# First feed-forward block on TensorE: operand places in SBUF, the order of its opening, and eight modulation sums in another stage

## The chip, the cores and the metric

The kernel runs on one core of a Trainium2 chip as one program. Five engines work beside each other: TensorE (PE, matmuls), VectorE (DVE), ScalarE (ACT), GpSimd (POOL) and SyncE (SP), whose queue starts nearly all loads. Each engine runs its own instructions in order and waits on semaphores for the others. SBUF holds 128 partitions; PSUM takes the matmuls' sums in banks. The metric is the time of one execution on the device in microseconds (us).

## The reference

The model has two layers on 512 tokens and a context of 256, with 1024 features. Layer 0 mixes with a Fourier and Hyena mixer, layer 1 with attention. Each layer ends in a gated feed-forward block (FFN) with a convolution of three taps:

```python
def _adaln(cond, w_mod, b_mod):
    mod = jax.nn.silu(cond) @ w_mod + b_mod
    return jnp.split(mod[:, None, :], 6, axis=-1)

def _conv_ffn(h, w_up, conv_w, conv_b, w_down):
    gate, val = jnp.split(h @ w_up, 2, axis=-1)
    return (jax.nn.silu(_dwconv3(gate, conv_w, conv_b)) * val) @ w_down

for i in range(DEPTH):
    sh1, sc1, g1, sh2, sc2, g2 = _adaln(c, w_mod[i], b_mod[i])
    ...
    x = x + g1 * yx
    x = x + g2 * _conv_ffn(_modulate(_rms_norm(x, norm2[i]), sh2, sc2), *ffn)
    if not last:
        ctx = ctx + cg1 * yc
        ctx = ctx + cg2 * _conv_ffn(_modulate(_rms_norm(ctx, norm2[i]), csh2, csc2), *ffn)
```

The change lies in the FFN of layer 0, over tokens and context together (768 columns), and in the modulation sums (`_adaln`) of layer 1, which are computed while that FFN runs. What is computed stays the same.

## The kernel before

Features lie on the partitions and tokens along the free axis. Every float32 product is made of three matmuls (`mm3`, lines 335 to 337): each operand is split into a high part (ACT, line 309) and the rest (DVE, line 314), and high x high, low x high and high x low are summed in a bank. So a moving operand has tiles named with h and l, and a weight tile likewise: `wh`/`wl` (1024 columns wide), `bh`/`bl` (512 wide).

`up0` is the FFN of layer 0. Its input after the norm is `h0h`, `h0l`, `h1h`, `h1l`: four feature blocks of 128 in each, 768 columns. There are 22 blocks of 128 hidden features. The first five are computed plainly, the later 17 with seven products per block instead of eight, in the manner of Strassen: feature halves and column halves (384 each) form two-by-two blocks, P1 to P7 are the products, and T1, T2, T4 (and T3 in place of `h0`'s second half) are sums of input blocks, made once on DVE. A product is twelve matmuls of 384 columns.

Hidden blocks are gathered in six groups (`GROUPS0`). For the first five, the down product (`DN`, `DL`) reads the activations `act0` to `act5` and the weights `bh`/`bl`, in matmuls of 384 columns, and is added to the residual in DRAM (`XA`, `XD`). The sixth group has six blocks and is written out in Python behind the table: its matmuls have 256 columns, its weights are `wh`/`wl` and `k3h` to `k7l`, and its outputs go to the residual tiles `xr` (line 1833), whose squares (line 444) and sums (line 451) form the next norm: column sums on PE (line 457), reciprocal root on DVE (lines 462 to 353), spreading on PE (line 475).

All engines follow an order that is written out: `UP0_ORDER` is a table of tokens, each the name of a step and its block. `LG` and `LV` load a block's gate and value weights; `HG`, `DG`, `H1`, `D1` and the like split weights; `S1` to `S4` form sums of weights; `CV` to `MU` are the convolution and the gate; `AH`, `AL` split the activation; `LW`, `HW`, `DW` load and split down weights. `LM:i` loads one row block of the modulation matrix into a raw buffer, and `GV:i` forms its sum on DVE (line 420 for each condition, then line 421). Raw buffers (`wr`, three, and `wx`, two) are shared by `LG`, `LV`, `LW` and `LM`; a step takes the buffer that became free first, and SP waits until its last reader is done. There are 56 modulation sums left when `up0` begins; the last 40 need one condition alone. The table has numbers 0 to 47; `GEMV0 = 48` says that the last eight are formed in the sixth group, by `more` between the outputs.

The opening of `up0` stands ahead of the table: two outputs, (0, q = 0) and (0, q = 1), eight pieces each, beside which the context's norm ends (`take`, `f2`, `a2`).

Where tiles lie follows from the order of allocation and from small pad tiles (`hpad`, `tpad`, `bpad`, `apad`). Places modulo 512 bytes, per partition: `h0` 64, `h1` 128, T1 192, T2 256, T4 320, `act0` to `act5` 128, 192, 256, 320, 384, 448; weights `wh`/`wl` and `k3` to `k7` 256; `bh`/`bl` 384, 448 and 0. In the second FFN the moving operands lie at 448 and the weights at 256.

Of the kernel before, what the change touches and what calls it, by code (L numbers as in the profile page):

```python
# [30 lines left out]
GEMV0 = 48  # L31
# [119 lines left out]
LV:1 LG:2 LV:2 XS:0 LM:0 LG:3 EA:0 GB:0 GV:0 LM:1 VB:0 HV:1 EB:0 DV:1 CV:0 LV:3 CX:0 GB:1 HG:2 GV:1 CC:0 LM:2 VA:1 DG:2 HV:2 SI:0 DV:2 LG:4 EA:1 EB:1  # L151
MU:0 LM:3 GV:2 AH:0 VB:1 AL:0 LV:4 GV:3 CV:1 SG:2 HG:3 CX:1 LM:4 DG:3 CC:1 LW:0.0 SI:1 GV:4 SV:2 HV:3 EB:2 MU:1 EA:2 LW:0.1 HW:0.0 DV:3 AH:1 AL:1 LM:5
DW:0.0 CV:2 LW:0.2 HW:0.1 CX:2 DW:0.1 CC:2 LG:5 SG:3 HG:4 GV:5 SI:2 HW:0.2 MU:2 LM:6 DG:4 AH:2 AL:2 LV:5 DW:0.2 LW:0.3 GV:6 SV:3 HV:4 EA:3 EB:3 CV:3
DV:4 LM:7 CX:3 LW:0.4 CC:3 SI:3 GV:7 SG:4 HG:5 MU:3 LM:8 DG:5 AH:3 AL:3 T1:0 GV:8 TH1:0 SV:4 EA:4 EB:4 CV:4 CX:4 LG:6 T2:0 CC:4 TH2:0 TL1:0 SI:4 T1:1
DN:0.0 DL:0.0 MU:4 TH1:1 T2:1 DN:0.1 XA:0.0 HW:0.3 XD:0.0 TL1:1 TH2:1 DW:0.3 T4:0 LV:6 DN:0.2 XA:0.1 TL2:0 HA:5 XD:0.1 TH4:0 T4:1 TL4:0 TH4:1 P1:5
HW:0.4 DA:5 XA:0.2 TL4:1 P2:5 E1:5 S1:5 XD:0.2 TL2:1 S3:5 DN:0.3 T3:0 AH:4 H1:5 D1:5 HA:6 XA:0.3 S2:5 P5:5 DW:0.4 LM:9 XD:0.3 S4:5 LW:0.5 T3:1 H4:5
P4:5 E5:5 HG:6 D4:5 TH3:1 TH3:0 TL3:1 P6:5 LM:10 TL3:0 HW:0.5 DG:6 DN:0.4 E2:5 GV:9 P3:5 DA:6 XA:0.4 LW:0.6 C1:5 XD:0.4 S1:6 DW:0.5 P7:5 S3:6 LM:11
C2:5 H1:6 S2:6 P1:6 E3:5 V2:5 HW:0.6 D1:6 P2:6 V1:5 LW:0.7 AL:4 GV:10 CV:5 P5:6 P4:6 DW:0.6 LG:7 CX:5 LM:12 DN:0.5 HW:0.7 S4:6 CC:5 H4:6 GV:11 SI:5
E1:6 HG:7 DN:0.6 XA:0.5 D4:6 LV:7 XD:0.5 MU:5 LW:1.0 C1:6 E5:6 DW:0.7 AH:5 P6:6 DG:7 LM:13 XA:0.6 HA:7 AL:5 XD:0.6 P3:6 E2:6 GV:12 HW:1.0 DN:0.7 C2:6
LW:1.1 DA:7 CV:6 GV:13 P7:6 XA:0.7 XD:0.7 HW:1.1 P1:7 CX:6 E3:6 LM:14 V2:6 CC:6 P2:7 V1:6 SI:6 S1:7 E1:7 MU:6 S3:7 AH:6 DW:1.0 H1:7 AL:6 DN:1.0 LW:1.2  # L160
D1:7 DL:1.0 S2:7 DW:1.1 LG:8 P5:7 XA:1.0 S4:7 LM:15 GV:14 H4:7 XD:1.0 P4:7 E5:7 HW:1.2 HG:8 D4:7 DN:1.1 LV:8 DW:1.2 LW:1.3 DG:8 LM:16 C1:7 P6:7 XA:1.1
GV:15 XD:1.1 HA:8 P3:7 E2:7 HW:1.3 DW:1.3 LW:1.4 DA:8 DN:1.2 LM:17 C2:7 S1:8 CV:7 GV:16 P7:7 XA:1.2 HW:1.4 XD:1.2 S3:8 LG:9 P1:8 E3:7 V2:7 H1:8 S2:8
# [12 lines left out]
H4:13 MU:12 LV:14 P2:13 E1:13 D4:13 AH:12 DN:3.0 AL:12 HG:14 LW:3.3 GV:31 DL:3.0 C1:13 LM:32 P5:13 XA:3.0 HW:3.2 XD:3.0 DW:3.2 P4:13 E5:13 LM:33 GV:32
P6:13 HA:14 DA:14 LW:3.4 S1:14 DN:3.1 E2:13 S3:14 GV:33 P3:13 XA:3.1 LG:15 HW:3.3 XD:3.1 DW:3.3 DN:3.2 H1:14 C2:13 LM:34 CV:13 D1:14 DG:14 P7:13
XA:3.2 CX:13 HW:3.4 XD:3.2 P1:14 E3:13 V2:13 S2:14 V1:13 LV:15 S4:14 P2:14 CC:13 H4:14 DW:3.4 E1:14 D4:14 LW:3.5 DN:3.3 SI:13 HG:15 MU:13 LM:35 DG:15
AH:13 P5:14 HA:15 GV:34 XA:3.3 C1:14 XD:3.3 LW:3.6 P4:14 E5:14 DA:15 GV:35 P6:14 HW:3.5 S1:15 LM:36 DW:3.5 S3:15 LW:3.7 DN:3.4 E2:14 AL:13 S2:15 S4:15
GV:36 P3:14 XA:3.4 HW:3.6 XD:3.4 LG:16 DW:3.6 P7:14 H1:15 C2:14 LV:16 CV:14 D1:15 P1:15 E3:14 V2:14 H4:15 LM:37 CX:14 P2:15 V1:14 CC:14 D4:15 SI:14
DN:3.5 E1:15 MU:14 LW:4.0 HG:16 C1:15 AH:14 DG:16 P5:15 HA:16 XA:3.5 AL:14 GV:37 XD:3.5 P4:15 E5:15 LM:38 DN:3.6 HW:3.7 DW:3.7 DA:16 LW:4.1 S1:16  # L180
S3:16 P6:15 XA:3.6 S2:16 GV:38 HW:4.0 XD:3.6 P3:15 E2:15 DW:4.0 LM:39 S4:16 LW:4.2 P7:15 H1:16 C2:15 CV:15 D1:16 DN:3.7 E3:15 V2:15 H4:16 LG:17 CX:15
V1:15 CC:15 P1:16 XA:3.7 D4:16 SI:15 XD:3.7 HW:4.1 P2:16 MU:15 LM:40 E1:16 DW:4.1 AH:15 GV:39 LV:17 P5:16 HG:17 AL:15 LW:4.3 DG:17 DN:4.0 E5:16 DL:4.0
C1:16 GV:40 P4:16 XA:4.0 LM:41 HW:4.2 XD:4.0 DW:4.2 DN:4.1 HA:17 LW:4.4 DA:17 S1:17 GV:41 P6:16 XA:4.1 S3:17 LM:42 HW:4.3 XD:4.1 S2:17 P3:16 DW:4.3
E2:16 S4:17 LG:18 DN:4.2 H1:17 C2:16 GV:42 CV:16 D1:17 LV:18 P7:16 XA:4.2 CX:16 LW:4.5 HW:4.4 XD:4.2 DW:4.4 P1:17 E3:16 V2:16 LM:43 H4:17 V1:16 CC:16
P2:17 D4:17 E1:17 SI:16 LW:4.6 MU:16 DN:4.3 HG:18 C1:17 AH:16 DG:18 GV:43 P5:17 HA:18 XA:4.3 DA:18 LM:44 AL:16 XD:4.3 P4:17 E5:17 S1:18 S3:18 P6:17
S2:18 HW:4.5 DW:4.5 S4:18 LW:4.7 GV:44 DN:4.4 E2:17 LG:19 P3:17 XA:4.4 HW:4.6 XD:4.4 DW:4.6 P7:17 H1:18 C2:17 LM:45 CV:17 D1:18 P1:18 E3:17 V2:17
# [66 lines left out]
class Builder:  # L253
# [1097 lines left out]
    def layer0(self):  # L1351
# [40 lines left out]
    def up0(self, x, H, hh, hl, steps, first, gl):  # L1392
# [30 lines left out]
        with self.tc.manual_schedule(engines={ENG.PE, ENG.DVE, ENG.Activation, ENG.SP, ENG.Pool}):  # L1423
# [1585 lines left out]
```

## Time and profile before

| what | us |
|---|---|
| three runs | 1535.95, 1524.69, 1538.45 |
| median | 1535.95 |
| the profiled execution's own time | 1526.98 |
| its span, first to last instruction | 1525.2 |

The span is cut into stages by the line and tile names: mixer up to about 340 us, opening and up stage of the first FFN to 831.6, its sixth group to 894.8, then attention and the second FFN. Matmuls are pipelined, and the profile's end of a matmul is modelled, so the pace of a row of matmuls is read from the spacing of their starts. A line of the views gives busy time of an instruction group, the mean of one, and the idle time of its engine ahead of it with what ended it. A wait is named by the engine that came last.

### The profile page before, as it was taken

How to read it: one execution, taken by the hardware profiler on the slowest of the kernel's cores; microseconds unless marked ns; L12 is line 12 of the kernel's file. 1: busy time of each engine (PE TensorE's matmuls, PEld its weight loads, DVE VectorE, ACT ScalarE, POOL GpSimd, SP SyncE). 2: the span in 40 equal slices, each digit the busy share in tenths (PEclk: the TensorE clock that was granted, in tenths of full speed). 3: DMA queues.
4: the chain of work that ended last, by engine and by line, in shares of the span. 5: the costliest groups of instructions: out<-in, count | busy, mean ns of one | idle time of the engine just before them, and what ended most of it. 6: DMA issues, size and time to landing. Idle time of an engine off the chain costs nothing.

```text
span 1525.2 us, 24578 instructions
## 1 busy us (share of the span) xinstructions
PE 1483.3 (97%) x9668; PEld 1346.8 (88%) x9668; DVE 1269.3 (83%) x2150; ACT 773.4 (51%) x1236; POOL 129.5 (8%) x150
## 2 busy tenths in 40 slices
PE   7999999999999999999999888999999999999998
PEld 4778888889999999999999877766558999999998
DVE  5799978888989898878787667999987899898883
ACT  4362235424445555555555235988964556555551
POOL 0022126000000111010100000111120000000000
PEclk9999999999999999999999989999999999999999
DMA  9336512454535767776763720000015123332322
GB/s 342 137 109 215 184 61 70 145 186 180 162 86 136 188 173 181 190 178 169 185 161 104 240 73 32 10 15 6 10 43 179 63 77 127 110 115 94 119 91 98
DMA packets 66370, 192.30 MB, mean 126 GB/s; under 512 B 7499, under 2 KB 14989, under 8 KB 65229
## 3 DMA queue, kind: packets, MB, share of 16 engines
q1 hardware_dynamic: 60493, 174.99, 34.4%
q0 software_dynamic: 5760, 15.73, 6.9%
q8 instruction: 76, 1.25, 0.3%
q14 instruction: 41, 0.34, 0.1%
HBM read 166.05 MB, written 24.64 MB: 125 GB/s over the span
## 4 chain that ended last, share of the span: by engine, by line
PE 85%; DVE 8%; ACT 2%; issue 2%; DMA 2%; POOL 1%; SPq 0%; ACTq 0%; DVEq 0%; POOLq 0%
PE bank L337 16%; PE bank L335 16%; PE bank L336 16%; PE mm L335 5%; PE mm L336 4%; PE mm L337 4%; PE pv L2282 3%; PE ms L337 3%; PE ms L335 3%; PE ms L336 3%; DVE junk L420 2%; PE s L335 2%; PE pv L2293 1%; PE s L337 1%; PE s L336 1%
## 5 line engine op out<-in xcount | busy, mean ns | idle before, releaser
L309 ACT ACTIVATE wh<-wr 128x1024 fp32r<-128x1024 f32 (+2 forms) x150 | 148.1, 989 | 167.1 <-PE bank L336 53.3
L314 DVE TENSOR_TENSOR wl<-wr,wh 128x1024 fp32r<-128x1024 f32 (+2 forms) x150 | 171.3, 1145 | 19.5 <-ACT wh L309 18.8
L335 PE MATMUL bank<-act,wh 128*128 128x256 f32 x406 | 113.3, 279 | 0.0
L337 PE MATMUL bank<-act,wl 128*128 128x256 f32 x406 | 113.2, 279 | 0.0
L336 PE MATMUL bank<-act,wh 128*128 128x256 f32 x406 | 113.0, 278 | 0.0
L420 DVE SCALAR_TENSOR_TENSOR junk<-wr,sb 128x1024 bf16<-128x1024 f32 x83 | 101.7, 1225 | 8.3 <-DMA wr<-wmodT 8.3
L337 PE MATMUL bank<-act,bl 128*128 128x384 f32 x256 | 86.5, 338 | 0.5 <-DVE bl L314 0.5
L336 PE MATMUL bank<-act,bh 128*128 128x384 f32 x256 | 86.4, 337 | 0.0
L335 PE MATMUL bank<-act,bh 128*128 128x384 f32 x256 | 86.1, 336 | 0.0
L337 PEld LDWEIGHTS bank<-act,wl 128*128 128x128 f32 x406 | 77.1, 190 | 0.1
L336 PEld LDWEIGHTS bank<-act,wh 128*128 128x128 f32 x406 | 77.1, 190 | 0.0
L335 PEld LDWEIGHTS bank<-act,wh 128*128 128x128 f32 x406 | 77.1, 190 | 0.0
L1773 POOL DMA_DIRECT2D xq<-st x40 | 34.8, 870 | 485.3 <-ACT st L1768 485.3
L337 PE MATMUL bank<-h0h,wl 128*128 128x384 f32 x216 | 72.8, 337 | 1.4 <-DVE wl L314 1.4
L335 PE MATMUL bank<-h0h,wh 128*128 128x384 f32 x216 | 72.8, 337 | 0.0
L336 PE MATMUL bank<-h0l,wh 128*128 128x384 f32 x216 | 72.6, 336 | 0.0
L2234 ACT ACTIVATE S<-s,rks 128x512 f32<-128x512 f32 x96 | 63.1, 688 | 12.7 <-PE s L337 6.3
L335 PE MATMUL mm<-hh,wh 128*128 128x512 f32 x152 | 62.5, 411 | 5.5 <-ACT wh L309 3.0
L336 PE MATMUL mm<-hl,wh 128*128 128x512 f32 x152 | 60.3, 397 | 2.3 <-DVE hl L490 2.3
L337 PE MATMUL mm<-hh,wl 128*128 128x512 f32 x152 | 60.3, 397 | 0.0
L2256 DVE TENSOR_TENSOR S<-S,mx 128x1536 f32<-128x1536 f32 x32 | 54.8, 1743 | 1.1 <-POOL mx L2252 1.1
L309 ACT ACTIVATE wh<-ss 128x1024 fp32r<-128x1024 f32 x36 | 38.2, 1062 | 33.9 <-PE bank L336 27.4
(677 smaller groups left out, 5130.6 us busy)
## 6 DMA issues: line engine op xcount, KB each, us to landing
wr<-w_up SPq DMA_DIRECT2D x75, 512.0 KB, 4.0
wr<-wmodT SPq DMA_DIRECT2D x62, 512.0 KB, 4.1
xq<-st POOLq DMA_DIRECT2D x40, 384.0 KB, 5.7
wx<-wmodT SPq DMA_DIRECT2D x18, 512.0 KB, 4.4
wr<-w_dx SPq DMA_DIRECT2D x24, 384.0 KB, 3.1
wm<-wmod0a SPq DMA_DIRECT2D x8, 1024.0 KB, 10.0
wr<-w_in SPq DMA_DIRECT2D x16, 512.0 KB, 3.9
wx<-w_up SPq DMA_DIRECT2D x13, 512.0 KB, 5.8
```

Of the source, the lines that this page charges most:

```text
L309: self.nc.scalar.activation(dst, src, AF.Copy)
L314: (eng or self.nc.vector).tensor_tensor(dst, src, hi.bitcast(F32), op=ALU.subtract)
L335: mmul(out, wh, xh, start=start, stop=False, **kw)
L336: mmul(out, wh, xl, start=False, stop=False, **kw)
L337: mmul(out, wl, xh, start=False, stop=stop, **kw)
L420: nc.vector.scalar_tensor_tensor(junk, raw, 1.0, self.sb[:, j, :], op0=ALU.mult, op1=ALU.mult, accum_out=acc)
L1773: nc.gpsimd.dma_start(xd[m], st[g, m], accum_op=ALU.add)
L2234: nc.scalar.activation(c.S[a, j // 3][:, j % 3, :], c.ps[a, j], AF.Copy, scale=c.s.r[:, g : g + 1])
L2256: v.tensor_tensor(c.S[a, h], c.S[a, h], mb.to_broadcast([P, 3, T]), op=ALU.subtract)
L2282: nc.tensor.matmul(c.P[64 * a : 64 * a + 64, :], V[:, j, o : o + 64], c.S[a, j // 3][:, j % 3, :], start=j == 0, stop=j == 5, tile_positio ...
L2293: nc.tensor.matmul(c.zz[o : o + 32, :], self.ones32, c.S[a, h][:, i, :], start=i == 0, stop=i == 2, tile_position=(0, o))
```

## The change

**Places.** The 64-byte pads between the halves of `h`, between T1, T2, T4, between the pairs of `bh`/`bl` and between the `act` tiles go; one pad of 192 bytes ahead of the `bh` tiles and one of 416 bytes behind the `act` tiles take their place. Afterwards all moving operands of this FFN (`h0`, `h1`, T1, T2, T4, `act0` to `act5`) lie at 64 modulo 512, and all its weights at 256.

```diff
-            if r:
-                self.t(hp, [P, 16], F32, "hpad")
             H.append([self.t(hp, [P, 4, TV], F32R, f"h{r}{s}") for s in "hl"])
...
                 for j in (1, 2, 4):
-                    self.t(tp, [P, 16], F32, f"tpad{j}")
                     TT[j] = [self.t(tp, [P, 4, W2], F32R, f"T{j}{s}") for s in "hl"]
...
+                self.t(wB, [P, 48], F32, "bpad")
                 for n in range(3):
-                    self.t(wB, [P, 16], F32, f"bpad{n}")
                     for s in ("bh", "bl"):
                         R[s].free.append(self.t(wB, [P, 512], F32R, f"{s}{n}"))
...
                 for n in range(6):
-                    self.t(ax, [P, 16], F32, f"apad{n}")
                     self.t(ax, [P, 2 * TV], F32R, f"act{n}")
-                self.t(ax, [P, 8], F32, "apad6")
+                self.t(ax, [P, 104], F32, "apad")
```

**The opening.** The loops change places: all eight pieces of the first output, then the second's, with the norm's steps at other pieces.

```diff
-            for k in range(KD):
-                for q in range(2):
+            for q in range(2):
+                for k in range(KD):
                     piece(ps[0, q, 0], 0, q, 0, [k])
-                if k == 0:
-                    take(KD)
-                if k == 2:
-                    f2(step=0)
-                if k == 6:
-                    f2(step=1)
+                    if (q, k) == (0, 0):
+                        take(KD)
+                    if (q, k) == (0, 4):
+                        f2(step=0)
+                    if (q, k) == (1, 5):
+                        f2(step=1)
```

PE at the start of `up0`, before (`wh_3686`/`wl_3687` are the first output's weights, `wh_3692`/`wl_3693` the second's; `nt` is the norm's sum of squares):

```order
L335 MATMUL bank_3723<-h0h_3031,wh_3686 128x384
L336 MATMUL bank_3723<-h0l_3032,wh_3686 128x384
L337 MATMUL bank_3723<-h0h_3031,wl_3687 128x384
L335 MATMUL bank_3724<-h0h_3031,wh_3692 128x384
L336 MATMUL bank_3724<-h0l_3032,wh_3692 128x384
L337 MATMUL bank_3724<-h0h_3031,wl_3693 128x384
L457 MATMUL ms_3737<-ones_3_71,nt_3552 128x1 x2
```

PE at the same place, after (`wh_3685`/`wl_3686` are the first output's weights):

```order
L335 MATMUL bank_3722<-h0h_3031,wh_3685 128x384
L336 MATMUL bank_3722<-h0l_3032,wh_3685 128x384
L337 MATMUL bank_3722<-h0h_3031,wl_3686 128x384
L457 MATMUL ms_3733<-ones_3_71,nt_3551 128x1 x2
L335 MATMUL bank_3722<-h0h_3031,wh_3685 128x384
L336 MATMUL bank_3722<-h0l_3032,wh_3685 128x384
```

The second output's weights no longer stand in the first six matmuls; the column sums moved up by three.

**The modulation sums.** `GEMV0`, `left` and `more` go, and the table has `LM` and `GV` up to 55. It is written out anew as a whole: the same steps otherwise, in another order in many places.

```diff
-GEMV0 = 48
...
-            left = list(range(GEMV0, len(gl)))
-
-            def more(n):
-                for i in left[:n]:
-                    GV(i)
-                    left.remove(i)
-                    if i + 2 < len(gl):
-                        LM(i + 2)
-
...
-                if m == 3:
-                    LM(left[0])
-                    LM(left[1])
-                more((0, 0, 0, 1, 1, 2, 2, 2)[m])
...
-C2:18 S3:20 CV:18 D1:19 P7:18 CX:18 XA:4.7 LV:21 XD:4.7 CC:18 P1:19 E3:18 V2:18 H4:19 V1:18 SI:18 D4:19 P2:19 E1:19 HA:21 MU:18 LW:5.0 DA:21 AH:18
...
+DA:20 P3:18 E2:18 GV:51 S1:20 LM:52 DN:4.7 H1:19 C2:18 S3:20 CV:18 D1:19 CX:18 LG:21 P7:18 XA:4.7 GV:52 XD:4.7 P1:19 CC:18 E3:18 LV:21 H4:19 V2:18
```

DVE in the sixth group, from the output before the last to the last output's sum of squares, before (`xr` with 512 columns are the residual adds, `junk` the modulation sums, line 428 the next norm's factor):

```order
L1833 SCALAR_TENSOR_TENSOR xr_1013_7959<-bank_3724,mod_4_73,xr_1013_7959 128x512
L451 TENSOR_TENSOR nt_8037<-nt_8037,nt_8293 128x512
L420 SCALAR_TENSOR_TENSOR junk_8296,gacc_8297<-wr_3690,sb_87 128x1024
L421 TENSOR_TENSOR mod_5_74<-gacc_8297,pcol_67 128x1
L420 SCALAR_TENSOR_TENSOR junk_8300,gacc_8301<-wr_3684,sb_87 128x1024
L421 TENSOR_TENSOR mod_5_74<-gacc_8301,pcol_67 128x1
L1833 SCALAR_TENSOR_TENSOR xr_1014_7960<-bank_3723,mod_4_73,xr_1014_7960 128x512
L428 SCALAR_TENSOR_TENSOR A_9_78<-mod_5_74,pcol_67 128x8
L1833 SCALAR_TENSOR_TENSOR xr_1007_7953<-bank_3725,mod_4_73,xr_1007_7953 128x256
L451 TENSOR_TENSOR nt_8037<-nt_8037,nt_8325 128x512
```

DVE at the same place, after:

```order
L1829 SCALAR_TENSOR_TENSOR xr_1017_7987<-bank_3721,mod_4_73,xr_1017_7987 128x512
L451 TENSOR_TENSOR nt_8065<-nt_8065,nt_8289 128x512
L1829 SCALAR_TENSOR_TENSOR xr_1018_7988<-bank_3723,mod_4_73,xr_1018_7988 128x512
L428 SCALAR_TENSOR_TENSOR A_9_78<-mod_5_74,pcol_67 128x8
L1829 SCALAR_TENSOR_TENSOR xr_1011_7981<-bank_3724,mod_4_73,xr_1011_7981 128x256
L451 TENSOR_TENSOR nt_8065<-nt_8065,nt_8313 128x512
```

The modulation sums between the adds are gone; all else stands in the same order.

SP from the last up weights to the first residual tiles (`xr`), before (`w_dy` with 768 columns are the sixth group's weights, `wmodT` the modulation rows):

```order
L1485 DMA wr_3696<-wmodT 128x1024
L1485 DMA wr_3696<-w_up 128x1024
L1485 DMA wr_3684<-w_up 128x1024
L1485 DMA wr_3690<-w_dy 128x768
L1485 DMA wx_810_3907<-w_dy 128x768
L1485 DMA wx_809_3906<-w_dy 128x768
L1485 DMA wr_3684<-w_dy 128x768
L1823 DMA xr_1007_7953<-xq_756_3709 128x768
```

SP at the same place, after:

```order
L1481 DMA wr_3689<-wmodT 128x1024 x2
L1481 DMA wx_805_3902<-w_up 128x1024
L1481 DMA wr_3689<-w_up 128x1024
L1481 DMA wx_806_3903<-wmodT 128x1024 x2
L1481 DMA wr_3695<-w_dy 128x768
L1481 DMA wr_3683<-wmodT 128x1024
L1481 DMA wx_806_3903<-w_dy 128x768
L1481 DMA wr_3683<-w_dy 128x768 x2
L1819 DMA xr_1011_7981<-xq_755_3708 128x768
```

Five modulation loads stand among the last weights where one stood, two pairs of them into one buffer after another, and the third and fourth load of the sixth group's weights share a buffer, ahead of the first residual tile.

More of the change, by code (lines that the diff above doesn't have):

```diff
@@ L191 @@
-P2:20 CC:19 V2:19 E1:20 SI:19 P5:20 C1:20 HG:21 MU:19 DG:21 AH:19 P4:20 E5:20 D4:20 AL:19 P6:20 LW:5.2 S2:21 S4:21 P3:20 E2:20 P7:20 H1:21 C2:20 CV:20
-D1:21 P1:21 H4:21 CX:20 E3:20 V1:20 P2:21 CC:20 D4:21 E1:21 SI:20 P5:21 V2:20 HW:5.0 C1:21 MU:20 P4:21 DW:5.0 E5:21 AH:20 AL:20 P6:21 P3:21 E2:21
-P7:21 HW:5.1 C2:21 CV:21 DW:5.1 CX:21 DN:5.0 HW:5.2 E3:21 DW:5.2 CC:21 V2:21 SI:21 DN:5.1 V1:21 MU:21 AH:21 AL:21 DN:5.2
+LV:1 LG:2 LV:2 XS:0 LM:0 LG:3 EA:0 GB:0 GV:0 VB:0 HV:1 LM:1 EB:0 DV:1 CV:0 LV:3 CX:0 CC:0 GB:1 HG:2 GV:1 SI:0 EA:1 MU:0 LM:2 VA:1 HV:2 DG:2 EB:1 DV:2
@@ L194 @@
+P4:20 E5:20 AL:19 S2:21 P6:20 GV:54 S4:21 LW:5.1 P3:20 E2:20 GV:55 LW:5.2 P7:20 H1:21 C2:20 CV:20 D1:21 P1:21 E3:20 CX:20 H4:21 V1:20 P2:21 CC:20
+D4:21 SI:20 E1:21 V2:20 P5:21 HW:5.0 C1:21 MU:20 DW:5.0 AH:20 P4:21 E5:21 AL:20 P6:21 P3:21 E2:21 P7:21 HW:5.1 C2:21 CV:21 DW:5.1 CX:21 DN:5.0 HW:5.2
+E3:21 DW:5.2 CC:21 V2:21 SI:21 V1:21 DN:5.1 MU:21 AH:21 AL:21 DN:5.2
 """
```

78 lines of the change are left out of this document (39 added, 39 removed).

## The prediction

> **What bounds the kernel now.** I read the page first: the total of each engine, then the slices, in which TensorE (PE) is full from the fifth slice to the end. The row of totals:
>
> ```profile
> PE 1483.3 (97%) x9668; PEld 1346.8 (88%) x9668; DVE 1269.3 (83%) x2150; ACT 773.4 (51%) x1236; POOL 129.5 (8%) x150
> ```
>
> PE sets the time, so a change pays only where it shortens PE's own work or takes away one of PE's waits. The next views are the busy times by stage (us of the stage, then busy us and count of PE, weight loads, VectorE (DVE), ScalarE (ACT), GpSimd, the granted clock, the DMA share) and, for 340 to 900 us, what PE waited for (total us, times, longest):
>
> ```profile
> 359.35:371.25 11.90, 10.49 (x62) 9.62 (x61) 6.89 (x20) 1.81 (x3) 0.00 (x0) 1.00 0.76 259
> 371.25:831.62 460.37, 459.83 (x2629) 459.45 (x2629) 387.86 (x642) 236.97 (x394) 34.80 (x40) 1.00 0.62 160
> 831.62:869.59 37.97, 37.97 (x325) 37.97 (x324) 26.09 (x46) 10.38 (x15) 0.00 (x0) 1.00 0.72 236
> 869.59:884.29 14.70, 7.47 (x38) 7.27 (x36) 9.17 (x29) 1.26 (x2) 0.00 (x0) 0.65 0.64 194
> ```
>
> ```profile
> PE ms L457 <- DVE nt L451: 7.2, 1, 7.2
> ...
> PE bank L337 <- DVE wl L314: 1.4, 2, 1.1
> PE bank L337 <- DVE bl L314: 0.5, 1, 0.5
> ```
>
> The stages are: the opening of the first FFN (first two products), its up stage, the last down group, and that group's end. The up stage is bound by PE without a gap (459.83 of 460.37). What can be won there is the pace of the matmuls. The group's end holds the one long wait, 7.2 us, and behind it a clock of 0.65. The two wl waits are the opening's.
>
> **The change part by part.**
>
> *The eight sums that leave the last group.* VectorE and PE at that wait:
>
> ```profile
> 842.78 0.88 DVE L1833 SCALAR_TENSOR_TENSOR xr<-bank,mod,xr 128x256 f32<-128x256 f32 x2 [3.09 <-PE bank L337]
> ...
> 872.18 1.22 DVE L420 SCALAR_TENSOR_TENSOR junk<-wr,sb 128x1024 bf16<-128x1024 f32 x1
> ...
> 873.52 1.22 DVE L420 SCALAR_TENSOR_TENSOR junk<-wr,sb 128x1024 bf16<-128x1024 f32 x1
> ...
> 874.86 0.74 DVE L1833 SCALAR_TENSOR_TENSOR xr<-bank,mod,xr 128x512 f32<-128x512 f32 x1
> ...
> 876.35 0.69 DVE L451 TENSOR_TENSOR nt<-nt,nt 128x512 f32<-128x512 f32 x1 [0.28 <-ACT nt L444]
> ...
> 879.00 0.16 DVE L462 TENSOR_SCALAR nrm_s<-ms 128x4 f32<-128x4 f32 x1 [1.56 <-PE ms L457]
> ...
> 881.18 0.16 DVE L353 SCALAR_TENSOR_TENSOR rq_r<-rq_b,rq_r 128x4 f32<-128x4 f32 x1
> ```
>
> ```profile
> 869.59 0.28 PE L337 MATMUL bank<-act,wl 128*128 128x256 f32 x1
> 877.10 1.86 PE L457 MATMUL ms<-ones,nt 128*128 128x1 f32 x8 [7.23 <-DVE nt L451]
> 878.82 0.56 PE L335 MATMUL bank<-act,wh 128*128 128x256 f32 x1
> ```
>
> One sum holds VectorE for 1.34 us (872.18 to 873.52). Eight are 10.7 us, and they stand ahead of the last residual add (L1833, 874.86) and the last square (L451, 876.35) that PE's column sums (L457) need. Without them the last add starts when PE has ended output 7: 869.7 less two context pieces of 18 matmuls at 117 ns (37.97 us over 324 matmuls) is 865.5. The add of the first context piece, ahead of L451, waits for PE until 867.6 and takes 0.5, so L451 runs from about 868.1 to 868.8, and PE comes to L457 at 869.7. The wait goes, with 0.9 us to spare.
>
> What is late next: the eight column sums, 1.72 us (877.10 to 878.82) at the slow clock, take about half, 0.86, and end at 870.6. VectorE's reciprocal root takes 2.34 (879.00 to 881.34) and starts 0.18 after them, so it ends at 873.1. PE's next piece of 18 ends at 872.7, so a wait of 0.4 is left; the eight spreading matmuls (L475) then take about as long as the sums, 0.8, and the rest begins at 873.9. Before, it began at 884.29. That is **-10.3 us**. What follows hangs on this point and moves with it.
>
> The eight loads leave SP's queue too, ahead of the loads for attention: nothing waited on those, so nothing is counted. At the front of the stage, though, SP's load of down weights 3 now goes into the buffer of weights 2. It was issued at 828; now it waits for the split of weights 2, and the residual tiles are queued behind it:
>
> ```profile
> 828.04 0.38 SPq L1485 DMA_DIRECT2D wr<-w_dy  x1
> ```
>
> ```profile
> 832.92 0.95 DVE L314 TENSOR_TENSOR wl<-wx,wh 128x768 fp32r<-128x768 f32 x1
> ```
>
> That split ends near 833.9, and the tiles' first use is the 842.78 above. With some 5 us to land, 3 to 4 us of cover remain: counted at nothing.
>
> *The same eight in the up stage.* VectorE rises from 387.9 to 398.6 us of 460 (87%). Cover is its 72 idle us and PE's own length. The one PE wait there is the 0.5 us for bl, at the end of a down group's chain. I take nothing, with bounds of -0.5 (that wait goes) and +10.7 (all eight bare).
>
> *The opening.* The first output's eight pieces now run before the second's. PE and VectorE there:
>
> ```profile
> 360.11 0.44 PE L337 MATMUL bank<-h0h,wl 128*128 128x384 f32 x1 [0.25 <-DVE wl L314]
> ...
> 362.30 0.45 PE L337 MATMUL bank<-h0h,wl 128*128 128x384 f32 x1 [1.12 <-DVE wl L314]
> ```
>
> ```profile
> 358.84 1.22 DVE L314 TENSOR_TENSOR wl<-wr,wh 128x1024 fp32r<-128x1024 f32 x1
> ...
> 361.03 2.35 DVE L314 TENSOR_TENSOR wl<-wr,wh 128x1024 fp32r<-128x1024 f32 x2
> ```
>
> The first wl is needed as before, so its wait stays. The second's (ready near 362.2) is needed four microseconds later and its wait goes. The stage holds 48 matmuls of 173 ns, 8.3 us, and some 1.1 us of small ones; with the first wait and its slow restart (0.5) that is 9.9 of 11.90. **-2.0 us.** The part of the normed tile that the last piece needs (VectorE, just before 361.03) is ready before PE gets there, seven pieces (3.6 us) and two small groups after 359.5.
>
> *The addresses.* Matmul ends are modelled, so I take the spacing of starts: each row is the first of twelve matmuls on that operand.
>
> ```profile
> 819.00 0.33 PE L335 MATMUL ms<-h1h,wh 128*128 128x384 f32 x1
> ...
> 821.10 0.34 PE L335 MATMUL bank<-T1h,wh 128*128 128x384 f32 x1
> ...
> 823.23 0.34 PE L335 MATMUL ms<-T4h,bh 128*128 128x384 f32 x1
> ...
> 825.34 0.34 PE L335 MATMUL bank<-T2h,wh 128*128 128x384 f32 x1
> ...
> 827.42 0.34 PE L335 MATMUL bank<-h1h,wh 128*128 128x384 f32 x1
> ...
> 829.54 0.33 PE L335 MATMUL bank<-h0h,wh 128*128 128x384 f32 x1
> ...
> 831.62 0.28 PE L335 MATMUL bank<-act,wh 128*128 128x256 f32 x1
> ```
>
> ```profile
> 756.14 0.33 PE L335 MATMUL bank<-act,bh 128*128 128x384 f32 x1
> ...
> 759.29 0.34 PE L335 MATMUL bank<-h1h,wh 128*128 128x384 f32 x1
> ```
>
> h0 lies at 64 modulo 512 with weights at 256 already: 2.08 us for twelve, 173.3 ns each. h1 (128) takes 2.10 and 2.12, T1 (192) 2.13, T4 (320) 2.11, T2 (256) 2.08; eighteen on act at mixed places take 3.15, where 18 of 173.3 are 3.12. After the change all have h0's places. By counts: 54 blocks of h1 x 0.03 = 1.6; 17 of T1 x 0.05 = 0.85; 17 of T4 x 0.03 = 0.5; T2 nothing; 768 matmuls on act are 42.7 blocks x 0.03 = 1.3. **-4.3 us**, all on PE's path.
>
> The last group's 432 matmuls of 256 columns get 64 too, and no row has 256 columns there. Nearest rows: these same matmuls at mixed places, 117.2 ns, and the second FFN, all at 448:
>
> ```profile
> 1500.15 0.28 PE L336 MATMUL bank<-act,wh 128*128 128x256 f32 x1
> ...
> 1504.23 0.28 PE L336 MATMUL bank<-act,wh 128*128 128x256 f32 x1
> ```
>
> Thirty-six take 4.08 us, 113.3 each. I take the same rows' 117.2, so nothing; the ends are -1.7 us (432 x 3.9 ns) and, as far on the other side, +1.7.
>
> [...]
>
> **Sum:** -10.3 - 2.0 - 4.3 = -16.6 us. Against the profiled execution's own 1526.98 us (span 1525.2) that is 1510.4. It lies 9.0 under the median of the runs shown (1524.69 to 1538.45); the mean of those three and the profiled one is 1531.5, and I forecast from that: 1515.
>
> **The rivals.**
>
> 1. *The places do nothing*: the blocks differ for another reason, such as which product follows which. Then -12.3, 1519. For it: T2 at 256 is as quick as h0. Against: h1 is slower than h0 in the same loop. [...]
>
> 2. *The sums are bare in the up stage.* For it: VectorE ends level with PE at the bl wait. Against: PE waited 0.5 us in 460. All eight bare give +10.7, in all -5.9: 1526; some of them, between that and 1515.
>
> 3. *The moved loads make it slower.* Modulation rows share five raw buffers and SP's queue with the weights:
>
> ```profile
> wr<-wmodT SPq DMA_DIRECT2D x62, 512.0 KB, 4.1
> ```
>
> Near the end of the up stage SP now has two such loads into one buffer behind each other, the second waiting for the first's sum, with weights queued behind. If each of the eight holds up weights that PE needs by 4.1 + 1.34 = 5.4 us, that costs 43.5, in all +26.9: 1558. It is slower than before from 16.6 / 8 = 2.1 us of bare delay for each. Against it: no row of PE's waits names a load in the up stage.
>
> **How the numbers follow.** Forecast 0.65, rival 1 0.12, rival 2 0.18, rival 3 0.05. About 1% (15 us) is what a measurement of this kernel can tell from no change. The forecast lies just past that line, so of its 0.65 I count 0.53 as faster by more and 0.12 within; of rival 1, 0.02 beyond and 0.10 within; rival 2 within; rival 3 slower. Faster 0.55, same 0.40, slower 0.05. Range: the fastest run less 16.6 and less 1.7 is 1506, the slowest less 16.6 is 1522, rival 2's end 1526: 1505 to 1526 leaves out rival 3 and runs off the mean.
>
> **What would show it.** Right: no PE wait at L457 after the last output, a clock of 1.00 there; twelve matmuls on h1, T1, T4 in 2.08 us; the second output's wl wait gone. Wrong: PE waits on wl, bl or act in the up stage, VectorE idle for a load of wmodT with weights late behind it, blocks of twelve still at 2.10 to 2.13, or 256 columns slower than 117 ns.

## The result and the profile after

The changed kernel takes 1516.34 us (median of 20 runs, 1509.28 to 1527.72) against 1535.77 us of the kernel before (20 runs beside them, 1524.69 to 1545.62): a ratio of 0.9887 with a 95% interval of 0.9861 to 0.9913, so 1.1% faster. Two single executions among all that follow took 2455 and 2963 us, far more than any other, and are left out of every figure. The changed kernel's profiled execution took 1521.48 us, its span is 1519.7. The row of totals:

```profile
PE 1486.3 (98%) x9668; PEld 1352.5 (89%) x9668; DVE 1270.9 (84%) x2150; ACT 773.8 (51%) x1236; POOL 129.6 (9%) x150
```

PE is busier than before (1483.3) in a shorter span. The busy times by stage say why. The stages are those shown of before; columns as there (us of the stage, then busy us and count of PE, weight loads, DVE, ACT, POOL, the granted clock):

```profile
357.05:367.24 10.19, 9.94 (x63) 9.62 (x62) 6.89 (x20) 1.80 (x3) 0.00 (x0) 1.00 0.77 243
367.24:822.77 455.53, 455.53 (x2630) 455.48 (x2629) 399.65 (x666) 237.06 (x394) 34.81 (x40) 1.00 0.64 170
822.77:860.81 38.04, 38.04 (x324) 38.04 (x324) 22.05 (x36) 11.65 (x17) 0.00 (x0) 1.00 0.70 235
860.81:865.22 4.41, 4.20 (x37) 4.00 (x36) 2.84 (x14) 0.00 (x0) 0.00 (x0) 1.00 0.00 0
```

| stage | before, us | after, us | difference | forecast |
|---|---|---|---|---|
| all ahead of the opening | 359.35 | 357.05 | -2.30 | 0 |
| opening | 11.90 | 10.19 | -1.71 | -2.0 |
| up stage | 460.37 | 455.53 | -4.84 | -4.3 |
| last group, to the rest behind L475 | 52.67 | 42.45 | -10.22 | -10.3 |
| that rest, attention, the first bit of the second FFN | 366.71 | 369.58 | +2.87 | 0 |
| the second FFN from there to the end of the span | 274.2 | 284.9 | +10.7 | 0 |

The three stages that the change touches lost 16.77 us, where 16.6 were forecast. But this pair of profiles differs by only 5.5 us in span: 2.3 us less ahead of the opening and 13.6 us more behind the last group, in code that the change does not touch. First the touched stages. What PE waited for at the end of the last group and at the opening, in 330 to 900 us:

```profile
PE bank L337 <- DVE wl L314: 0.2, 1, 0.2
PE ms L475 <- DVE rq_r L353: 0.2, 1, 0.2
```

The 7.2 us at L457, the second wait on wl and the 0.5 us for bl in the up stage are gone; 0.2 is left ahead of L475. The rows of DVE and of PE there:

```profile
856.89 0.75 DVE L1829 SCALAR_TENSOR_TENSOR xr<-bank,mod,xr 128x512 f32<-128x512 f32 x1 [2.05 <-PE bank L337]
...
859.41 0.68 DVE L451 TENSOR_TENSOR nt<-nt,nt 128x512 f32<-128x512 f32 x1
```

```profile
860.93 0.95 PE L457 MATMUL ms<-ones,nt 128*128 128x1 f32 x8
...
864.31 1.16 PE L475 MATMUL ms<-cst,rq_r 128*128 128x128 f32 x8 [0.21 <-DVE rq_r L353]
865.22 0.36 PE L335 MATMUL bank<-act,k3h 128*128 128x256 f32 x1
```

DVE now waits for PE (2.05 us ahead of the last residual add of 512 columns), no longer the other way round. The sum for L457 ends at 860.09, and PE comes there at 860.93: 0.84 us to spare, with the clock at 1.00 where it was 0.65. In the up stage each row below is the first of twelve matmuls of 384 columns:

```profile
797.81 0.34 PE L335 MATMUL bank<-T1h,wh 128*128 128x384 f32 x1
...
799.89 0.34 PE L335 MATMUL ms<-T4h,bh 128*128 128x384 f32 x1
...
801.97 0.34 PE L335 MATMUL bank<-T2h,wh 128*128 128x384 f32 x1
...
804.05 0.34 PE L335 MATMUL bank<-h1h,wh 128*128 128x384 f32 x1
...
806.13 0.34 PE L335 MATMUL bank<-h0h,wh 128*128 128x384 f32 x1
```

All take 2.08 us, 173.3 ns per matmul; 2628 of them are the whole stage, so nothing is left to win there but the pace. Now the second FFN, one row of the busy times from the kernel before and one from the changed one:

```profile
1251.00:1521.00 270.00, 270.00 (x2384) 270.00 (x2383) 221.43 (x326) 134.89 (x212) 0.00 (x0) 1.00 0.32 106
```

```profile
1234.80:1515.50 280.70, 280.70 (x2385) 280.70 (x2384) 222.57 (x326) 135.41 (x212) 0.00 (x0) 1.00 0.30 102
```

The same matmuls of 256 columns, with operands at the same places modulo 512 (448, weights 256), no wait and a clock of 1.00 in both: 113.3 ns each before, 117.7 after. The place where the pace of the changed kernel turns is one late weight. Its split on DVE, and PE:

```profile
1233.77 0.68 DVE L314 TENSOR_TENSOR wl<-wr,wh 128x512 fp32r<-128x512 f32 x1
```

```profile
1234.26 0.28 PE L335 MATMUL bank<-act,wh 128*128 128x256 f32 x1
1234.37 0.28 PE L336 MATMUL bank<-act,wh 128*128 128x256 f32 x1
1234.50 0.38 PE L337 MATMUL bank<-act,wl 128*128 128x256 f32 x1
1234.73 0.28 PE L335 MATMUL bank<-act,wh 128*128 128x256 f32 x1
1234.84 0.28 PE L336 MATMUL bank<-act,wh 128*128 128x256 f32 x1
```

The split ends at 1234.45. Up to there the starts are 113.3 ns apart (1234.26 to 1234.37); the matmul on wl comes about 0.02 us late, its successor 0.11 us more, and from then on every start is 117.8 ns behind the last, for 2385 matmuls, to the end. The kernel before has the same little hitch at the same matmul and comes out of it at 113.3. The changed kernel's 20 runs lie in two groups, 10 from 1509.3 to 1514.5 us and 10 from 1518.2 up, and the profiles say that this pace decides the group. Of the eleven profiled executions with the moved sums (this one and those below), the four that end at 117.8 ns took 1521.5 to 1524.9 us, and of the seven that end at 113.3 six took 1509.4 to 1515.4 (the seventh, 1520.8, is accounted for below). The runs of the kernel before can be parted in two likewise, but all three of its profiles, two of them variants below, are quick, so that its upper group is the same thing is not shown. The 2.87 us go with the clock: in two spells of some 3.4 us each at the start of attention it was half, which it was not in the profile of before. The last section shows one. Ahead of the opening it is the other way round: the profile of before has such a spell at 232 us, the other none there.

### The profile page after: what moved, and what is told of

The parts are those of the page before. It is cut to its first block, busy times and chain, and to the rows that moved or that the text cites. A ratio compares the mean times of both kernels' runs of the same rounds, so it can differ in the third digit from the quotient of the medians.

```text
span 1519.7 us, 24581 instructions
## 1 busy us (share of the span) xinstructions
PE 1486.3 (98%) x9668; PEld 1352.5 (89%) x9668; DVE 1270.9 (84%) x2150; ACT 773.8 (51%) x1236; POOL 129.6 (9%) x150
## 4 chain that ended last, share of the span: by engine, by line
PE 88%; DVE 6%; ACT 2%; issue 1%; POOL 1%; DMA 1%; SPq 0%; DVEq 0%; ACTq 0%; POOLq 0%
PE bank L335 17%; PE bank L337 17%; PE bank L336 17%; PE mm L335 4%; PE mm L336 4%; PE mm L337 4%; PE pv L2265 3%; PE ms L337 3%; PE ms L335 3%; PE ms L336 3%; PE s L335 2%; PE pv L2276 1%; PE s L337 1%; PE s L336 1%; DVE junk L420 1%
## 5 line engine op out<-in xcount | busy, mean ns | idle before, releaser
L420 DVE SCALAR_TENSOR_TENSOR junk<-wr,sb 128x1024 bf16<-128x1024 f32 x70 | 86.9, 1241 | 11.1 <-DMA wr<-wmodT 11.0
L420 DVE SCALAR_TENSOR_TENSOR junk<-wx,sb 128x1024 bf16<-128x1024 f32 x42 | 51.2, 1220 | 6.1 <-DMA wx<-wmodT 6.1
```

The source lines that it names most:

```text
L420: nc.vector.scalar_tensor_tensor(junk, raw, 1.0, self.sb[:, j, :], op0=ALU.mult, op1=ALU.mult, accum_out=acc)
```

## The experiments

Three questions: do the parts bring what their terms say, each by itself; is it the address that sets the pace of the up stage; and what sets the pace of the second FFN.

**Each part alone.** The addresses alone: the pads of the change in the kernel before.

```diff
-            if r:
-                self.t(hp, [P, 16], F32, "hpad")
...
-                    self.t(tp, [P, 16], F32, f"tpad{j}")
...
+                self.t(wB, [P, 48], F32, "bpad")
...
-                self.t(ax, [P, 8], F32, "apad6")
+                self.t(ax, [P, 104], F32, "apad")
```

> The kernel before with the addresses of the changed kernel (all moving operands of the first FFN at 64 modulo 512, all weights at 256) and nothing else. Theory, the place sets the pace: twelve matmuls of 384 columns on any operand take 2.08 us, the up stage goes from 460.4 to about 456 us, the wait of PE at L457 in the last group (7.2 us) stays, and the time is about 4 us lower. Rival, the blocks differed for another reason: 460.4 us and no change of the time.

Opening and up stage of that kernel, and its waits:

```profile
359.60:371.46 11.86, 10.44 (x62) 9.58 (x61) 6.88 (x20) 1.80 (x3) 0.00 (x0) 1.00 0.76 260
371.46:827.85 456.39, 455.82 (x2630) 455.37 (x2629) 387.78 (x642) 236.81 (x394) 34.82 (x40) 1.00 0.61 162
```

```profile
PE ms L457 <- DVE nt L451: 8.2, 1, 8.2
```

The up stage is 3.98 us shorter, as the theory has it, the opening is untouched. The wait at L457 grew by 1.0 us: DVE, whose eight sums set that end, leaves the shorter up stage later against PE than before (its last L451 ends 46.4 us after the group's start, where it was 45.4). Of 4.0 us won 0.6 are given back (53.26 us from the last group's start to the rest, against 52.67). The runs give a ratio of 0.997 (0.9939 to 1.0001): the times alone can't tell it from nothing, the stage can. Rival 1, in which the places do nothing, is out by these 3.98 us.

The sums alone: the changed kernel with the old pads and the old opening.

```diff
+            if r:
+                self.t(hp, [P, 16], F32, "hpad")
...
-            for q in range(2):
-                for k in range(KD):
+            for k in range(KD):
+                for q in range(2):
```

> The changed kernel with the old addresses and the old opening: only the eight modulation sums are moved. Theory, they are hidden in the up stage: that stage stays at 460.4 us within 0.5, the wait at L457 is gone, the stretch from the last product of the last group's eighth output to its end is 10 us shorter, and the time is about 10 us lower. Rival, they are bare in the up stage: it grows by up to 10.7 us and the time stays where it was.

```profile
357.30:370.79 13.49, 12.08 (x63) 11.21 (x61) 7.00 (x20) 1.81 (x4) 0.00 (x0) 0.87 0.83 303
370.79:830.12 459.33, 459.33 (x2629) 459.10 (x2629) 399.78 (x666) 237.11 (x394) 34.80 (x40) 1.00 0.62 165
```

The up stage holds 11.9 us more of DVE's work (399.8 against 387.9) and is 1.0 us shorter, not longer. It was expected to stay within 0.5: the wait on bl is gone with the new table, which is 0.5 of it or a little more, and the rest is spread over the blocks. From the last group's start to the rest it takes 42.35 us, 10.3 less than before. The times: 0.9894 (0.9845 to 0.9942). The rival with bare sums is out. The opening, 13.49, is 1.6 longer than before at the same two waits; that is the clock (0.87 in the row), and comes back below.

The opening alone: the loops exchanged in the kernel before, the second edit of the change and nothing else.

```diff
-            for k in range(KD):
-                for q in range(2):
+            for q in range(2):
+                for k in range(KD):
```

> The kernel before with the new loop order of the opening alone. Theory: the opening goes from 11.9 us to 10.1 (the second wait on wl goes, the first stays), the up stage stays at 460.4 and the wait at L457 at about 7 us; about 2 us lower in all, too little for the timed runs. Rival, the shorter opening of the changed kernel came from the addresses: 11.9 us still.

```profile
357.19:367.43 10.24, 9.99 (x63) 9.67 (x61) 6.91 (x20) 1.82 (x3) 0.00 (x0) 1.00 0.72 249
```

10.24 us against 11.90, and 460.35 in the up stage: as the theory has it, 0.1 us short. The times, 0.9978 (0.9951 to 1.0005), can't tell it from nothing, as was expected.

**The address or the likeness of addresses.** All moving operands of the first FFN 128 bytes higher:

```diff
+            if not r:
+                self.t(hp, [P, 32], F32, "hpad")
...
-                self.t(wB, [P, 48], F32, "bpad")
+                self.t(wB, [P, 16], F32, "bpad")
...
-                self.t(ax, [P, 104], F32, "apad")
+                self.t(ax, [P, 72], F32, "apad")
```

> The changed kernel with every moving operand of the first FFN 128 bytes higher, at 192 modulo 512 in place of 64; weights stay at 256. Theory, it is the place itself that counts, and 192 is as slow for all as it was for T1 (12 matmuls in 2.126 us, 177.2 ns each): the up stage goes from 455.5 to 455.5 + 2628 x 3.9 ns = 465.8 us. Rival, what counts is that all operands lie at one and the same place: 173.3 ns each and 455.5 us still.

The up stage took 458.26 us: neither theory. The trace shows both of them, one after the other. First of twelve matmuls each:

```profile
463.64 0.34 PE L335 MATMUL bank<-T1h,wh 128*128 128x384 f32 x1
...
465.72 0.34 PE L335 MATMUL ms<-T4h,bh 128*128 128x384 f32 x1
...
467.80 0.34 PE L335 MATMUL bank<-T2h,wh 128*128 128x384 f32 x1
```

```profile
480.38 0.34 PE L335 MATMUL ms<-h1h,wh 128*128 128x384 f32 x1
...
482.47 0.33 PE L335 MATMUL bank<-T1h,wh 128*128 128x384 f32 x1
...
484.57 0.34 PE L335 MATMUL bank<-act,bh 128*128 128x384 f32 x1
```

Up to 467.80 us twelve take 2.08 at 192 as they did at 64; from there on they take 2.09 to 2.10, 174.7 ns each, to the end of the stage, T1 as well as h0. So 192 is not by itself the slow place that T1's 2.126 us had made it: one place has two paces, and no block at 192 took the 2.126 that T1 took among the mixed places. The turn has its moment: the matmul on `wl` in that block on T2 has its weights loaded from 468.04, 0.06 us late, behind the split on DVE. In the changed kernel the same load is 0.06 us late too (467.31), and there, at 64, the 173.3 ns stayed. The times, 0.9885 (0.9832 to 0.9939), say nothing on 2.7 us.

The act buffers alone at 448, the rest at 64:

```diff
-                self.t(ax, [P, 104], F32, "apad")
+                self.t(ax, [P, 136], F32, "apad")
```

> The changed kernel with the act buffers of the first FFN at 448 modulo 512, all other moving operands still at 64. Theory, a pace holds as long as all operands lie alike, and each step from one place to another can disturb it: the up stage is longer than 455.5 us, by about the 1.3 us that act was counted for, and the 256-column matmuls of the last group go at 113.4 or 117.8 by the break ahead of them. Rival, every place has its own pace: 113.3 ns in the last group, as the second FFN at 448 had in the kernel before, and the stage 455.5 if 448 is as good as 64.

```profile
368.37:824.79 456.42, 456.42 (x2629) 456.42 (x2629) 399.37 (x666) 237.44 (x394) 34.80 (x40) 1.00 0.62 169
```

0.9 us longer than with all at 64 (its single time is 1513.5 us), with no wait in it: two places among the operands cost a little, where the first theory named 1.3. But they do not cost it as that theory has it, by disturbing the pace at each step. The first matmuls of three blocks in a row:

```profile
459.99 0.34 PE L335 MATMUL bank<-act,bh 128*128 128x384 f32 x1
...
464.18 0.34 PE L335 MATMUL bank<-T1h,wh 128*128 128x384 f32 x1
...
466.26 0.34 PE L335 MATMUL ms<-T4h,bh 128*128 128x384 f32 x1
```

The 24 on act take 4.19 us, 174.6 ns each, the twelve on T1 2.08. So it is throughout the stage: each of the 38 blocks on act goes at 174.6 to 174.8 ns, all others at 172.8 to 173.7, and the pace changes from block to block with no late operand. Within this execution the pace does go with the place, as the prediction had it. In the last group, though, the 256-column matmuls at 448 went at 117.8 ns up to L475 and at 113.4 behind it, so the rival of one pace per place is out there. In all nine profiles with everything at 64 the stage kept 173.3 ns, across waits of up to 0.6 us. Whether 64 is a good place or only likeness counts, one profile each at 192 and 448 doesn't settle.

**The pace of the second FFN.** Two kernels have four added matmuls ahead of the second product of output 6, behind the late weight shown above:

```diff
         def P2(f):
             cd[f, 0] = self.ms()
+            if f == 6:
+                for n in range(4):
+                    nc.tensor.matmul(cd[f, 0][:, 256:384], self.ident, self.ident, start=True, stop=True)
```

> The changed kernel with four added matmuls of 128 columns (float32, the form of L475, into 128 unused columns of a bank) in the second FFN, ahead of the second product of its output 6, some 2300 matmuls of 256 columns before the end; nothing reads them. Theory, a stream of matmuls keeps the pace that its last break gave it, and a break of this form gives the quick one: all of the second FFN behind the added four at 113.3 ns, none at 117.8, and every run near the lower group of the changed kernel's times (1509 to 1515 us). Rival, the pace belongs to the execution: both 113.3 and 117.8 are met behind the four, and the times fall into two groups 10 us apart as before.

The other has four of one column:

```diff
+                    nc.tensor.matmul(cd[f, 0][:, 256 + n : 257 + n], self.ident, self.ones32[:, 0:1], start=True, stop=True)
```

> The same place in the changed kernel, but the four added matmuls have one column each (the form of L457). Theory: a break of this form leaves the slow pace behind it: 117.8 ns to the end, and every run near the upper group of times (1518 to 1524 us). Rival, the pace belongs to the execution: two groups of times, 10 us apart.

All six runs of each lie in the lower group: 1510.8 to 1515.8 us and 1509.5 to 1514.1, ratios to before of 0.9855 (0.982 to 0.9891) and 0.9849 (0.9816 to 0.9881). So a break does decide it, but its form does not: the small one, which was to leave the slow pace, leaves the quick one. That four matmuls turn a slow stream quick is read from these times (18 of the changed kernel's own 32 runs are in the lower group, all twelve here); in both profiles the stream came to them at 113.3 ns and stayed there. The next kernel has four breaks in one execution:

```diff
+            if f in (9, 17):
+                for n in range(4):
+                    nc.tensor.matmul(cd[f, 0][:, 256:384], self.ident, self.ident, start=True, stop=True)
+            if f in (6, 13):
+                for n in range(4):
+                    nc.tensor.matmul(cd[f, 0][:, 256 + n : 257 + n], self.ident, self.ones32[:, 0:1], start=True, stop=True)
```

> The changed kernel with four such breaks in the second FFN: the form of one column ahead of the second product of outputs 6 and 13, the form of 128 columns ahead of that of outputs 9 and 17. Theory: the spacing of starts goes 117.8, 113.3, 117.8, 113.3 ns from break to break. Rivals: it stays what it was at the first break (the pace belongs to the execution), or it changes with no regard to the form (it is drawn anew at each).

113.3 to 113.4 ns behind all four, as ahead of the first: again the form has no say, but the rival of a pace kept from the first break on fits this one execution as well. (Its single time, 1520.8 us, is high for another reason: 4.7 us more than the changed kernel's profile from the end of the first FFN through attention.) Then one added matmul in place of four:

```diff
+            if f == 6:
+                nc.tensor.matmul(cd[f, 0][:, 256:257], self.ident, self.ones32[:, 0:1], start=True, stop=True)
```

> The changed kernel with one added matmul of one column (into an unused column of a bank, read by nothing) ahead of the second product of the second FFN's output 6. Theory, any break behind the last wait leaves the quick pace: 113.3 ns behind it, all runs in the lower group, about 0.3 us less than with four added matmuls. Rival, it was the length of the break (0.47 us with four) and one is too short: two groups.

and, beside it on the same chip, the changed kernel again:

> The changed kernel itself once more, beside the three below on one chip. Theory: its times fall into two groups again, near 1512 and near 1521 us, as the wait on wl in the second FFN's first down product leaves the matmuls behind it at 113.3 or 117.8 ns. Rival, the two groups were those of other chips or hours: one group.

The changed kernel again had two groups, 8 runs from 1507.2 to 1512.3 and 4 from 1520.0 to 1523.0 (0.9891, 0.9856 to 0.9925). With one added matmul all twelve lie in the upper group, 1517.6 to 1524.9 (0.9937, 0.9911 to 0.9964). So neither theory nor rival: one matmul left the slow pace in every run, four the quick one. The profile with one comes to it at 117.8 ns already; that of the next experiment comes at 113.3 and goes on at 117.8, so one matmul does turn the stream. The same stretch of 252 us in the second FFN, with four added matmuls of one column, then with one:

```profile
1248.00:1500.00 252.00, 252.00 (x2226) 252.00 (x2225) 210.19 (x310) 129.69 (x203) 0.00 (x0) 1.00 0.31 106
```

```profile
1248.00:1500.00 252.00, 252.00 (x2142) 252.00 (x2142) 208.32 (x307) 128.66 (x202) 0.00 (x0) 1.00 0.31 105
```

PE is full in both, and does 84 matmuls less in the second: 113.2 against 117.6 ns.

A second such matmul, in the last group of the first FFN:

```diff
+                    if m == 3:
+                        nc.tensor.matmul(p[:, 0:1], self.ident, self.ones32[:, 0:1], start=True, stop=True)
```

> The kernel with one added matmul in the second FFN, and one more in the last group of the first FFN, ahead of the fourth output's product, 215 matmuls of 256 columns before the column sums of L457. Theory, a break gives the quick pace there too: 113.4 in place of 117.8 ns, the stage 0.9 us less 0.2 for the break. Rival, at 64 modulo 512 matmuls of 256 columns go at 117.8 whatever comes before (as in all stretches of the last group at 64 so far): 0.2 us more.

The matmuls of the last group behind it stay at 117.8 ns and the stage is 0.2 us longer, as the rival says. But one matmul leaves the slow pace in the second FFN too, and two profiles (the changed kernel again, and the last experiment below) have 113.3 ns at 64 behind L475: the place does not hold the pace at 117.8. Four were not tried there. All twelve runs are in the upper group again (1519.1 to 1523.4).

The last experiment missed its aim:

```diff
-LW:0.1 E5:4 DN:0.0 E2:4 HG:5 T3:1 DL:0.0 TH3:0 HA:5 D4:4 TH3:1 P4:4 HW:0.1 TL3:0 P3:4 TL3:1 DG:5 P7:4 S1:5 C1:4 P1:5 E3:4 S2:5 DA:5 H1:5 P2:5 S4:5
+LW:0.1 E5:4 E2:4 HG:5 T3:1 TH3:0 HA:5 D4:4 TH3:1 P4:4 DN:0.0 DL:0.0 HW:0.1 TL3:0 P3:4 TL3:1 DG:5 P7:4 S1:5 C1:4 P1:5 E3:4 S2:5 DA:5 H1:5 P2:5 S4:5
```

> The changed kernel with the second FFN's first down product (DN and DL of group 0, output 0) one product later in the order, behind P4 of output 4, 1.4 us: its wl is ready by then, nothing is added. Theory, the wait on that wl is what sets the pace of all that follows, and without it the pace stays as the stretch ahead has it: the wait is gone from the trace, and all times are in the lower group if that stretch goes at 113.3, in the upper one if it goes at 117.7. Rival, the wait has nothing to do with it: two groups, 1512 and 1521.

The late weight is not that of the product moved (output 0 of the group) but of output 2, `DN:0.2`, a block later; its hitch stays in the trace. The times (four from 1510.2 to 1511.6, one of 1522.0) are those of the changed kernel. That taking the late weight away fixes the pace was thus not tried. The other half of the theory, that the pace of the stretch ahead goes on, does not hold: in this profile the matmuls ahead of the late weight go at 117.8 ns and those behind it at 113.3. Over all 14 profiles the seven that come to it at 117.8 all leave it at 113.3; of the seven that come at 113.3 four leave at 113.3 and three at 117.8.

## Why the prediction came out right

The forecast was 1515 us, with the time 1516.3: inside the range, and in "faster by over 1%", its likeliest case (the interval, down to 0.9% faster, reaches across that line). Point by point:

- *The sums leave the last group, -10.3*: -10.22 in the changed kernel, -10.3 with the sums alone. The inner steps hold too: 0.84 us to spare at L457 (0.9 forecast), a left-over wait of 0.2 at L475 (0.4), the rest 42.45 us after the stage's start (42.3).
- *The same eight in the up stage, 0*: they cost nothing there, and the sums bare in that stage, rival 2, are out. With the sums alone the stage was 1.0 us shorter, 0.5 beyond the lower bound, as the new order took away the wait on bl. No PE wait names a load: the moved loads, rival 3, did nothing.
- *The opening, -2.0*: -1.71, and -1.66 alone. The second wait went and the first stayed; the term was 0.3 too large.
- *The places, -4.3*: -3.98 alone (the stage's -4.84 holds the wait on bl besides). By the spacing of starts that is h1 1.4 (forecast 1.6), T1 0.6 (0.85), T4 0.3 (0.5), act 1.4 (1.3), and T2 0.2, which was put at nothing from one quick block. The size was right, the reason only in part. That step of the prediction took the slower blocks as what their own address costs (128, 192, 320), and bounded the last group by the 113.3 ns of the second FFN, as if they were a mark of 448. At 192 the runs showed 173.3 and 174.7 ns at one address, at 448 113.3 and 117.8; with act alone at 448 the pace did follow the address. What the pads removed is the mixture, and why a mixture is slower stays open. The 256 columns at 64 went at 117.8 up to L475 in every profile with that place, within the bounds.
- *The base, 1531.5*: this was the weak term. It was a mean over four executions of a kernel whose times lie in two groups, 36 runs from 1523.7 to 1533.0 (mean 1527.8) and 44 from 1534.6 to 1546.1 (1538.8), over all 80 runs taken here. Only 1.6 us lie between the two, so the line is drawn, not seen. The changed kernel's 32 runs do likewise: 18 with a mean of 1510.8, 14 with 1521.4. Group for group the change is worth 17.0 and 17.4 us, which agrees with the sum of 16.6. The medians differ by 19.4, more than any step explains (the means by 17.3), as the groups' shares differ between the two samples. The base was 4.3 under the median measured beside the changed kernel and the difference of medians 2.8 over the sum; that the two offset each other, and the forecast came within 1.3 us, is luck.

One of the signs that the prediction named for being wrong was met: 256 columns "slower than 117 ns". In the last group it was 117.8, worth 0.1 us against before (38.04 us for 37.97). In the second FFN it was 117.8 too, worth 10.7, and had nothing to do with the change.

Of the kernels run, the changed one with four added matmuls in the second FFN is the best: all twelve runs of the two forms have a mean of 1512.3 us, where the changed kernel's 32 have 1515.4. The two were not run side by side on one chip.

## What to carry to other kernels

Compare two kernels stage by stage from the first matmul of each stage on, before the spans: here a gain of 16.8 us stood in two profiles as 5.5, as one of them had drawn the slower pace in code that the change does not touch. Where run times fall into two groups, look for one long stream of equal matmuls and compare its spacing of starts between profiles; a few spare matmuls behind the last late operand settled it on the quick side here, one alone on the slow side, so their number has to be tried. Work on an engine that is behind at a stage's end is worth its full time there and nothing in a stage with cover: the same eight sums cost 10 us in one and 0 in the other.

## What the hardware showed beside it

- **Two paces of one stream.** Matmuls of 256 columns went at 113.3 or 117.8 ns, with the same operands, a clock of 1.00 and no wait; in these streams, with operands at one place, the pace turned only at a break (an operand or weight late by as little as 0.02 us, small matmuls) and then held for up to 2385 matmuls. Some breaks left the same pace in all 14 profiles (behind the second FFN's first spreading at L475 113.3 ns, behind the column sums at L457 ahead of it 117.8), the late weight of `DN:0.2` left either. At 384 columns the two were 173.3 and 174.7; with two places mixed the pace changed there from block to block with no break (172.8 to 173.7 and 174.6 to 174.8). Which property of a break decides is open: one added matmul of one column and four differ, four of 1 and of 128 columns do not.
- **The clock after short waits.** The opening has the same two waits on wl, 1.4 us together, in the kernel before and with the sums alone. Two slices of 2 us of the kernel before, then three of the other; the column ahead of the last two is the granted clock:

```profile
361.00:363.00 2.00, 0.88 (x8) 0.70 (x6) 2.00 (x3) 0.00 (x0) 0.00 (x0) 1.00 0.77 254
363.00:365.00 2.00, 2.00 (x13) 2.00 (x13) 0.45 (x2) 0.00 (x0) 0.00 (x0) 1.00 0.85 248
```

```profile
359.00:361.00 2.00, 0.89 (x5) 0.74 (x4) 2.00 (x3) 0.00 (x0) 0.00 (x0) 0.86 0.90 262
361.00:363.00 2.00, 2.00 (x8) 2.00 (x8) 0.50 (x2) 0.00 (x0) 0.00 (x0) 0.50 0.81 252
363.00:365.00 2.00, 2.00 (x12) 2.00 (x12) 0.00 (x0) 0.00 (x0) 0.00 (x0) 0.78 0.96 348
```

The one kept its clock; the other had half of it for 3.4 us (0.14, 0.50 and 0.22 of three slices of 2 us lost, over 0.5), which is the 1.6 us of its longer opening. At the start of attention the changed kernel's profile has the like behind a wait of 2.4 us, where that of before has the same wait and 1.00:

```profile
920.00:922.00 2.00, 1.53 (x5) 1.53 (x6) 1.34 (x3) 0.10 (x1) 0.00 (x0) 0.55 0.00 0
922.00:924.00 2.00, 2.00 (x9) 1.92 (x7) 0.00 (x0) 0.00 (x0) 0.00 (x0) 0.60 0.00 0
```

A wait of 1.1 or 2.4 us thus cost its own length in one execution, and 1.6 or 2.9 us more in another (the 2.9 with a second spell, from 927.0 to 930.4 us). What differs, as far as the profiles show, is where it falls. In each of the 14 profiles all spells begin on one grid of 3.41 us, which lies otherwise against the program from execution to execution; in those of before and of the changed kernel a spell lasts 3.41, 6.83 or 10.24 us. The step of that grid that holds the opening's first wait, before (where the second wait runs on into the next step) and then with the sums alone (where both waits lie in it):

```profile
358.58:361.99 3.41, 2.31 (x13) 1.44 (x11) 3.41 (x6) 2.20 (x3) 0.00 (x0) 1.00 0.21 50
```

```profile
357.07:360.48 3.41, 2.00 (x10) 1.13 (x9) 3.41 (x5) 1.71 (x3) 0.00 (x0) 1.00 0.42 111
```

PE was busy for 68% of the one and 59% of the other, and only the other was followed by half the clock; at the start of attention it was 49% before and 38% in the changed kernel. Over all profiles, from 345 to 1500 us and at full clock, each of the 21 steps with PE busy for under 43% was followed by half the clock, 3 of 6 with 43 to 50%, 2 of 25 with 50 to 60%, and 9 of 4630 above that. Those nine, all behind a step of full work at the start of attention, stay unexplained.
